# Batch normalisation at inference: stores on ScalarE's queue, one transfer at a time on each ring

## The chip, the cores and the metric

The kernel runs on one core of a Trainium2 chip. The metric is the device time of one execution in microseconds (us). A core has several engines that run side by side: ScalarE (ACT), VectorE (DVE), GpSimd (POOL), SyncE (SP) and TensorE, which has no work here. Sixteen DMA engines move data between the chip's main memory (HBM) and the core's on-chip memory of 128 partitions. An engine issues a transfer on a queue of its own; in the DMA engines that queue is a ring, and the profile numbers the rings q1 (SyncE), q10 (ScalarE) and q0 (GpSimd).

## The reference

```
x: float32 [32, 256, 128, 128]      gamma, beta, mean, var: float32 [256]
out = gamma * (x - mean) / sqrt(var + 1e-5) + beta        (per channel)
```

For each channel this is one multiplication and one addition: `scale = gamma / sqrt(var + eps)`, `shift = beta - mean * scale`, `out = x * scale + shift`. The input has 536.9 MB and the output as much.

## The kernel before

The 256 channels make two blocks of 128, one channel to a partition. An image and a block give a tile of 128 rows with 128 x 128 = 16384 numbers each, 64 KB a row and 8.4 MB a tile. There are 32 x 2 = 64 tiles (`NT`). Three buffers of that size (`bufs`, `NBUF = 3`) lie in on-chip memory; tile `i` uses buffer `i % 3`, and the result is written over the input in place.

At the start SyncE issues the first tile in two halves, with the four small parameter loads between them, and then tiles 1 and 2 (L89 to L98). VectorE and ScalarE work out `scale_t` and `shift_t` (L108 to L127). The main work is written out by hand, engine by engine:

- SyncE issues the loads of tiles 3 to 63 in order (L158 to L163). Load `i` waits on `stored[s]`, the semaphore that the store of tile `i - 3` raises when it has left the buffer.
- ScalarE applies scale and shift to the whole tile in one instruction (`scalar_part`, L142) when it has landed, for all tiles but the first and the last.
- GpSimd issues the stores of tiles 0 to 60 (L172), each when ScalarE has finished its tile (`adone`). The last three stores (`NTAIL`) are issued by ScalarE.
- VectorE (`vector_part`, L131) does the left half of tile 0 and the first 9216 columns of tile 63, and nothing in between.

Nothing else orders the transfers: a load may stand on its ring behind another load, a store behind another store. At the end GpSimd and SyncE wait for all stores.

Of the kernel before, what the change touches and what calls it, by code (L numbers as in the profile page):

```python
# [8 lines left out]
NBUF = 3  # L9
PAD = 936  # L10
NHEAD = 3
NTAIL = 3
VHEAD = 8192
VLAST = 9216


@with_exitstack
def kernel(
    ctx: ExitStack,
    tc: tile.TileContext,  # L20
    x: bass.AP,
    gamma: bass.AP,
    beta: bass.AP,
    running_mean: bass.AP,
    running_var: bass.AP,
    out: bass.AP,
):
    nc = tc.nc
    eps = 1e-5
    f32 = mybir.dt.float32  # L30

    N, C, H, W = x.shape
    P = nc.NUM_PARTITIONS
    assert C % P == 0
    NCB = C // P
    HW = H * W
    NT = N * NCB
    B = 32
    NQ = P // B
    NE = 16  # L40
    NPAR = 4

    xr = x.rearrange("n (cb p) h w -> (n cb) p (h w)", p=P)
    outr = out.rearrange("n (cb p) h w -> (n cb) p (h w)", p=P)

    params = ctx.enter_context(tc.tile_pool(name="params", bufs=1))
    data = ctx.enter_context(tc.tile_pool(name="data", bufs=1))
    params.tile([P, PAD], f32, name="pad", tag="pad")
    bufs = [data.tile([P, HW], f32, name=f"t{s}", tag=f"t{s}") for s in range(NBUF)]
    rows = params.tile([B, NPAR * C], f32, name="rows", tag="rows")  # L50
    turned = params.tile([B, NPAR * C], f32, name="turned", tag="turned")
    par = params.tile([P, NPAR, NCB], f32, name="par", tag="par")
    eps_t = params.tile([P, 1], f32, name="eps_t", tag="eps")
    std_t = params.tile([P, NCB], f32, name="std_t", tag="std")
    rstd_t = params.tile([P, NCB], f32, name="rstd_t", tag="rstd")
    scale_t = params.tile([P, NCB], f32, name="scale_t", tag="scale")
    ms_t = params.tile([P, NCB], f32, name="ms_t", tag="ms")
    shift_t = params.tile([P, NCB], f32, name="shift_t", tag="shift")

    loaded = [tc.alloc_semaphore(f"loaded{s}") for s in range(NBUF)]
    stored = [tc.alloc_semaphore(f"stored{s}") for s in range(NBUF)]
    closed = [tc.alloc_semaphore(f"closed{s}") for s in range(NBUF)]
    early = tc.alloc_semaphore("early")
    first = [tc.alloc_semaphore(f"first{s}") for s in range(NHEAD)]
    vdone = tc.alloc_semaphore("vdone")
    adone = tc.alloc_semaphore("adone")
    fetched = tc.alloc_semaphore("fetched")
    vec = tc.alloc_semaphore("vec")  # L70
    act = tc.alloc_semaphore("act")

    with tc.tile_critical():  # L73
        count = [0]

        def step(inst, sem=None, value=None):
            if sem is not None:
                inst._wait_ge(sem, value)
            elif count[0]:
                inst._wait_ge(vec, count[0])  # L80
            inst.then_inc(vec, 1)
            count[0] += 1
            return count[0]

        left, right = slice(0, HW // 2), slice(HW // 2, HW)
        last = NT - 1


        nc.sync.dma_start(out=bufs[0][:, left], in_=xr[0][:, left]).then_inc(early, 16)  # L89
        zeroed = step(nc.vector.memset(rows[:], 0.0))  # L90
        for r, ap in enumerate((running_var, gamma, beta, running_mean)):
            inst = nc.sync.dma_start(out=rows[0:NE, r * C : (r + 1) * C], in_=ap.partition_broadcast(NE))  # L92
            if r == 0:
                inst._wait_ge(vec, zeroed)
            inst.then_inc(fetched, 16)
        nc.sync.dma_start(out=bufs[0][:, right], in_=xr[0][:, right]).then_inc(first[0], 16)  # L96
        for i in range(1, NHEAD):
            nc.sync.dma_start(out=bufs[i][:], in_=xr[i]).then_inc(first[i], 16)  # L98

        def landed(i):  # L100
            if i < NHEAD:
                return first[i], 16
            s = i % NBUF
            before = 1 if s < NHEAD else 0
            return loaded[s], 16 * (i // NBUF + 1 - before)


        step(nc.vector.memset(eps_t[:], eps))  # L108
        step(nc.vector.transpose(out=turned[:], in_=rows[:]), fetched, 16 * NPAR)  # L109
        blocks = turned.rearrange("p (rc q b) -> p rc q b", q=NQ, b=B)  # L110
        flat = par.rearrange("p r cb -> p (r cb)")
        for q in range(NQ):
            placed = step(nc.vector.tensor_copy(out=flat[q * B : (q + 1) * B], in_=blocks[:, :, q, 0]))  # L113
        var_t, gamma_t, beta_t, mean_t = (par[:, r] for r in range(NPAR))
        nc.scalar.activation(  # L115
            out=std_t[:],
            in_=var_t,
            func=mybir.ActivationFunctionType.Sqrt,
            bias=eps_t[:],
            scale=1.0,  # L120
        )._wait_ge(vec, placed).then_inc(act, 1)
        step(nc.vector.reciprocal(out=rstd_t[:], in_=std_t[:]), act, 1)  # L122
        step(nc.vector.tensor_mul(out=scale_t[:], in0=gamma_t, in1=rstd_t[:]))  # L123
        step(nc.vector.tensor_mul(out=ms_t[:], in0=mean_t, in1=scale_t[:]))  # L124
        ready = step(nc.vector.tensor_sub(out=shift_t[:], in0=beta_t, in1=ms_t[:]))  # L125
        nc.vector.wait_ge(vec, ready)
        nc.scalar.wait_ge(vec, ready)  # L127

        def vector_part(i, first_col, end):
            t, cb = bufs[i % NBUF], i % NCB  # L130
            return nc.vector.tensor_scalar(  # L131
                out=t[:, first_col:end],
                in0=t[:, first_col:end],
                scalar1=scale_t[:, cb : cb + 1],
                scalar2=shift_t[:, cb : cb + 1],
                op0=mybir.AluOpType.mult,
                op1=mybir.AluOpType.add,
            ).then_inc(vdone, 1)

        def scalar_part(i, first_col):  # L140
            t, cb = bufs[i % NBUF], i % NCB
            return nc.scalar.activation(  # L142
                out=t[:, first_col:],
                in_=t[:, first_col:],
                func=mybir.ActivationFunctionType.Identity,
                bias=shift_t[:, cb : cb + 1],
                scale=scale_t[:, cb : cb + 1],
            ).then_inc(adone, 1)


        def share(i):
            return VHEAD if i == 0 else VLAST if i == last else 0

        vector_part(0, 0, HW // 2)._wait_ge(early, 16)
        vector_part(last, 0, VLAST)._wait_ge(*landed(last))


        for i in range(NHEAD, NT):  # L158
            s = i % NBUF
            inst = nc.sync.dma_start(out=bufs[s][:], in_=xr[i])  # L160
            if i >= NBUF:
                inst._wait_ge(stored[s], 16 * (i // NBUF))
            inst.then_inc(loaded[s], 16)  # L163

        for i in range(NT):
            eng = nc.gpsimd if i < NT - NTAIL else nc.scalar
            packet = {"single_packet": True} if i < NT - NTAIL else {}
            written = (stored if i < NT - NTAIL else closed)[i % NBUF]
            scalar_part(i, share(i))._wait_ge(*landed(i))
            if i in (0, last):  # L170
                eng.wait_ge(vdone, 1 if i == 0 else 2)
            eng.dma_start(out=outr[i], in_=bufs[i % NBUF][:], **packet)._wait_ge(adone, i + 1).then_inc(  # L172
                written, 16
            )


        for s in range(NBUF):
            nc.gpsimd.wait_ge(stored[s], 16 * ((NT - NTAIL - s + NBUF - 1) // NBUF))
        nc.gpsimd.drain()

        for s in range(NBUF):
            nc.sync.wait_ge(stored[s], 16 * ((NT - NTAIL - s + NBUF - 1) // NBUF))
            nc.sync.wait_ge(closed[s], 16)


# [28 lines left out]
```

## Time and profile before

| | |
|---|---|
| median of 3 runs | 2508.89 us (2481.34 to 2515.49) |
| span of the profiled execution | 2479.7 us |
| ScalarE busy | 885.6 us (36%), 66 instructions |
| VectorE busy | 13.1 us (1%), 13 instructions |
| GpSimd busy | 32.7 us (1%), 65 instructions |
| moved by DMA | 1073.84 MB, 433 GB/s on average |
| load, issue to landing | 55.3 us (median of 63) |
| store from GpSimd, issue to landing | 46.2 us (median of 61) |

The span runs from the first to the last instruction of the profiled execution. That execution has no other time on record; the lowest of the three runs is 1.6 us above its span. "Busy" counts instructions that compute; the issue of a transfer is not counted on SyncE and ScalarE. Issue to landing includes the time for which a transfer stands on its ring behind the one before it.

### The profile page before, as it was taken

How to read it: one execution, taken by the hardware profiler on the slowest of the kernel's cores; microseconds unless marked ns; L12 is line 12 of the kernel's file. 1: busy time of each engine (PE TensorE's matmuls, PEld its weight loads, DVE VectorE, ACT ScalarE, POOL GpSimd, SP SyncE). 2: the span in 40 equal slices, each digit the busy share in tenths (PEclk: the TensorE clock that was granted, in tenths of full speed). 3: DMA queues.
4: the chain of work that ended last, by engine and by line, in shares of the span. 5: the costliest groups of instructions: out<-in, count | busy, mean ns of one | idle time of the engine just before them, and what ended most of it. 6: DMA issues, size and time to landing. Idle time of an engine off the chain costs nothing.

```text
span 2479.7 us, 276 instructions
## 1 busy us (share of the span) xinstructions
DVE 13.1 (1%) x13; ACT 885.6 (36%) x66; POOL 32.7 (1%) x65
## 2 busy tenths in 40 slices
DVE  1000000000000000000000000000000000000000
ACT  2342432424424234242342433424334243342432
POOL 0000000000000000000000000000000000000000
DMA  9999999999999999999999999999999999999999
GB/s 410 437 440 426 437 440 428 434 440 432 430 440 432 430 440 433 429 440 436 427 440 436 427 440 437 426 440 437 426 440 437 426 440 438 425 440 438 425 440 406
DMA packets 18707, 1073.84 MB, mean 433 GB/s; under 512 B 2128, under 2 KB 2192, under 8 KB 2192
## 3 DMA queue, kind: packets, MB, share of 16 engines
q1 hardware_dynamic: 9488, 536.94, 50.0%
q0 software_dynamic: 8784, 511.71, 47.6%
q10 hardware_dynamic: 432, 25.17, 2.3%
q14 instruction: 3, 0.02, 0.0%
HBM read 536.94 MB, written 536.87 MB: 433 GB/s over the span
## 4 chain that ended last, share of the span: by engine, by line
another core or an unknown queue 61%; ACT 35%; DMA 2%; issue 0%; SPq 0%; DVE 0%; ACTq 0%; DVEq 0%
ACT t L142 35%; DMA t<-in_x_dram 2%; SPq L92 0%; DVE rows L90 0%; ACTq L172 0%; SPq L96 0%; DVE eps_t L108 0%; DVEq L209 0%; SPq L73 0%
## 5 line engine op out<-in xcount | busy, mean ns | idle before, releaser
L142 ACT ACTIVATE t<-t,shift_t,scale_t 128x16384 f32<-128x16384 f32 (+1 forms) x64 | 884.0, 13813 | 1554.8 <-DMA t<-in_x_dram 1554.8
L172 POOL DMA_DIRECT2D out_dram<-t x61 | 32.5, 534 | 2314.4 <-ACT t L142 2314.4
L131 DVE TENSOR_SCALAR t<-t,scale_t,shift_t 128x8192 f32<-128x8192 f32 (+1 forms) x2 | 9.6, 4812 | 2427.1 <-DMA t<-in_x_dram 2427.0
L115 ACT ACTIVATE std_t<-par,eps_t 128x2 f32<-128x2 f32 x1 | 0.3, 295 | 14.0 <-DVE par L113 14.0
L115 ACT ACT_TABLE_LOAD x1 | 1.3, 1283 | 0.9 <-SPq L73 0.9
L109 DVE STREAM_TRANSPOSE turned<-rows 32x1024 f32<-32x1024 f32 x1 | 1.2, 1233 | 11.9 <-DMA rows<-in_running_mean_dram 11.9
L90 DVE MEMSET rows<- 32x1024 f32 x1 | 0.9, 912 | 1.2 <-SPq L73 1.2
L113 DVE COPY par<-turned 32x8 f32<-32x8 f32 x4 | 0.6, 162 | 0.1
L122 DVE RECIPROCAL rstd_t<-std_t 128x2 f32<-128x2 f32 x1 | 0.2, 166 | 0.4 <-ACT std_t L115 0.4
L124 DVE TENSOR_TENSOR ms_t<-par,scale_t 128x2 f32<-128x2 f32 x1 | 0.2, 163 | 0.0
L125 DVE TENSOR_TENSOR shift_t<-par,ms_t 128x2 f32<-128x2 f32 x1 | 0.2, 161 | 0.0
L123 DVE TENSOR_TENSOR scale_t<-par,rstd_t 128x2 f32<-128x2 f32 x1 | 0.2, 160 | 0.0
L198 POOL MEMSET const-float32-0.0<- 128x1 f32 x1 | 0.1, 98 | 0.2 <-issue 0.2
L198 POOL MEMSET const-bfloat16-1.0<- 128x1 bf16 x1 | 0.1, 101 | 0.0
L198 POOL MEMSET const-float32-1.0<- 128x1 f32 x1 | 0.1, 98 | 0.0
L198 POOL MEMSET const-uint8-127<- 128x1 uint8 x1 | 0.1, 98 | 0.0
L108 DVE MEMSET eps_t<- 128x1 f32 x1 | 0.1, 59 | 0.1
## 6 DMA issues: line engine op xcount, KB each, us to landing
t<-in_x_dram SPq DMA_DIRECT2D x2, 4096.0 KB, 15.9
t<-in_x_dram SPq DMA_DIRECT2D x63, 55.3
out_dram<-t POOLq DMA_DIRECT2D x61, 46.2
out_dram<-t ACTq DMA_DIRECT2D x3, 32.2
rows<-in_running_var_dram SPq DMA_DIRECT2D x1, 16.0 KB, 11.3
rows<-in_gamma_dram SPq DMA_DIRECT2D x1, 16.0 KB, 11.1
rows<-in_beta_dram SPq DMA_DIRECT2D x1, 16.0 KB, 10.8
rows<-in_running_mean_dram SPq DMA_DIRECT2D x1, 16.0 KB, 10.7
```

What stands on the lines that cost most here:

```text
L90: zeroed = step(nc.vector.memset(rows[:], 0.0))
L109: step(nc.vector.transpose(out=turned[:], in_=rows[:]), fetched, 16 * NPAR)
L113: placed = step(nc.vector.tensor_copy(out=flat[q * B : (q + 1) * B], in_=blocks[:, :, q, 0]))
L115: nc.scalar.activation(out=std_t[:], in_=var_t, func=mybir.ActivationFunctionType.Sqrt, bias=eps_t[:], scale=1.0,)._wait_ge(vec, placed).t ...
L122: step(nc.vector.reciprocal(out=rstd_t[:], in_=std_t[:]), act, 1)
L123: step(nc.vector.tensor_mul(out=scale_t[:], in0=gamma_t, in1=rstd_t[:]))
L124: step(nc.vector.tensor_mul(out=ms_t[:], in0=mean_t, in1=scale_t[:]))
L125: ready = step(nc.vector.tensor_sub(out=shift_t[:], in0=beta_t, in1=ms_t[:]))
L131: return nc.vector.tensor_scalar(out=t[:, first_col:end], in0=t[:, first_col:end], scalar1=scale_t[:, cb : cb + 1], scalar2=shift_t[:, cb ...
L142: return nc.scalar.activation(out=t[:, first_col:], in_=t[:, first_col:], func=mybir.ActivationFunctionType.Identity, bias=shift_t[:, cb : ...
L172: eng.dma_start(out=outr[i], in_=bufs[i % NBUF][:], **packet)._wait_ge(adone, i + 1).then_inc(written, 16)
L198: nc = _bacc.Bacc("TRN2", target_bir_lowering=False, num_devices=1)
```

## The change

Three things change, and one follows from them.

1. All stores are issued by ScalarE, on its ring; GpSimd issues none, and the separate semaphores for the last three stores go. `gone(i)` names the semaphore and the value that say that tile `i` is stored.
2. VectorE takes part in each tile from tile 1 on: first columns 0 to 2559 (`VFIRST`), which raises `vfirst`, then columns 2560 to 14335 (`VMOST`; to 9215 for the last tile), which raises `vdone`. ScalarE does the rest, the last 2048 columns. A store waits for both engines.
3. From tile 3 on, SyncE issues load `i` when tile `i - 3` is stored and when VectorE has done the first part of tile `i - 1`, which means that load `i - 1` has landed. ScalarE starts its part of tile `i` only when tile `i - 1` is stored, for all tiles but the first and the last two. So in most of the run the load ring holds one load and the store ring one store.

```diff
-NTAIL = 3
+VFIRST = 2560
+VMOST = 14336
...
-        def share(i):
-            return VHEAD if i == 0 else VLAST if i == last else 0
-
-        vector_part(0, 0, HW // 2)._wait_ge(early, 16)
-        vector_part(last, 0, VLAST)._wait_ge(*landed(last))
+        def gone(i):
+            return stored[i % NBUF], 16 * (i // NBUF + 1)
+
+        vector_part(0, 0, VHEAD)._wait_ge(early, 16).then_inc(vdone, 1)
+        for i in range(1, NT):
+            vector_part(i, 0, VFIRST)._wait_ge(*landed(i)).then_inc(vfirst, 1)
+            vector_part(i, VFIRST, VLAST if i == last else VMOST).then_inc(vdone, 1)
 
         for i in range(NHEAD, NT):
             s = i % NBUF
-            inst = nc.sync.dma_start(out=bufs[s][:], in_=xr[i])
-            if i >= NBUF:
-                inst._wait_ge(stored[s], 16 * (i // NBUF))
-            inst.then_inc(loaded[s], 16)
+            nc.sync.wait_ge(*gone(i - NBUF))
+            nc.sync.dma_start(out=bufs[s][:], in_=xr[i])._wait_ge(vfirst, i - 1).then_inc(loaded[s], 16)
 
         for i in range(NT):
-            eng = nc.gpsimd if i < NT - NTAIL else nc.scalar
-            packet = {"single_packet": True} if i < NT - NTAIL else {}
-            written = (stored if i < NT - NTAIL else closed)[i % NBUF]
-            scalar_part(i, share(i))._wait_ge(*landed(i))
-            if i in (0, last):
-                eng.wait_ge(vdone, 1 if i == 0 else 2)
-            eng.dma_start(out=outr[i], in_=bufs[i % NBUF][:], **packet)._wait_ge(adone, i + 1).then_inc(
-                written, 16
+            if 0 < i < NT - 2:
+                nc.scalar.wait_ge(*gone(i - 1))
+            scalar_part(i, VHEAD if i == 0 else VLAST if i == last else VMOST)._wait_ge(*landed(i))
+            nc.scalar.wait_ge(vdone, i + 1)
+            nc.scalar.dma_start(out=outr[i], in_=bufs[i % NBUF][:])._wait_ge(adone, i + 1).then_inc(
+                stored[i % NBUF], 16
             )
```

More of the change, by code (lines that the diff above doesn't have):

```diff
@@ L137, in vector_part @@
                 op1=mybir.AluOpType.add,
-            ).then_inc(vdone, 1)
+            )
         def scalar_part(i, first_col):
```

10 lines of the change are left out of this document (3 added, 7 removed).

## The prediction

> **What bounds the kernel now.** I read the page's counts and queues first, then the instruction groups by shape, then the queue's own waits, then single windows.
>
> ```profile
> span 2479.7 us, 276 instructions
> DVE 13.1 (1%) x13; ACT 885.6 (36%) x66; POOL 32.7 (1%) x65
> DMA packets 18707, 1073.84 MB, mean 433 GB/s; under 512 B 2128, under 2 KB 2192, under 8 KB 2192
> q1 hardware_dynamic: 9488, 536.94, 50.0%
> q0 software_dynamic: 8784, 511.71, 47.6%
> q10 hardware_dynamic: 432, 25.17, 2.3%
> ```
>
> The last three lines give, for each ring, the share of the span of all 16 DMA engines that its packets took: loads on SyncE's ring q1 50.0%, GpSimd's stores on q0 47.6%, the last three stores on ScalarE's ring q10 2.3%. The sum is 99.9%. No compute engine is busy for over 36%. The DMA engines have 0.1% of 2479.7, some 2.5 us, left to win; more would need the same bytes to go faster than 433 GB/s.
>
> ```profile
> 100.00:2300.00 2200.00, 0.00 (x0) 797.95 (x58) 30.28 (x57) 1.00 1.00 434
> 4.00:31.00 27.00, 7.08 (x10) 7.51 (x2) 0.00 (x1) 1.00 1.03 438
> 0.00:1.00 1.00, 0.00 (x0) 0.09 (x1) 0.20 (x4) 1.00 0.00 0
> 1.00:2.00 1.00, 0.78 (x1) 1.00 (x1) 0.00 (x0) 1.00 0.49 131
> 2.00:3.00 1.00, 0.19 (x2) 0.19 (x1) 0.00 (x0) 1.00 1.26 393
> ```
>
> These are windows; the last two columns are DMA share and GB/s (a packet is counted where it starts, so short windows overshoot). Over 2200 us the share is 1.00 with both rings filled. From 4 to 31 us loads run alone, and one ring moves 438 GB/s: a lone ring gets the whole of the engines. The first three windows price a restart: the first load is issued at 0.96, no byte moves before 1.0 and the rate is there only within the third window, so issue to flow takes 1.0 to 1.8 us.
>
> ```profile
> SPq L160 <- DMA out_dram<-t: 2369.7, 61, 69.4
> ACT t L142 <- DMA t<-in_x_dram: 1554.8, 64, 27.2
> t<-in_x_dram SPq DMA_DIRECT2D x63, 55.3
> out_dram<-t POOLq DMA_DIRECT2D x61, 46.2
> ```
>
> SyncE's queue waits for stores to free a buffer, ScalarE for loads. A buffer's round is 55.3 (load) + 14.0 (compute) + 46.2 (store) = 115.5 us for three tiles, 38.5 a tile; successive computes in the trace stand 38.6 apart. So a load overlaps its successor on its ring by 55.3 - 38.6 = 16.7 us and a store by 7.6: neither ring ever runs dry, and that is why 99.9% is reached.
>
> **The change, part by part.** *Compute.*
>
> ```profile
> L142 ACT ACTIVATE t<-t,shift_t,scale_t 128x16384 f32<-128x16384 f32 x62 | 870.5, 14040 | 1525.3 <-DMA t<-in_x_dram 1525.3
> L142 ACT ACTIVATE t<-t,shift_t,scale_t 128x8192 f32<-128x8192 f32 x1 | 7.2, 7212 | 7.0 <-DMA t<-in_x_dram 7.0
> L142 ACT ACTIVATE t<-t,shift_t,scale_t 128x7168 f32<-128x7168 f32 x1 | 6.4, 6360 | 22.6 <-DMA t<-in_x_dram 22.6
> L131 DVE TENSOR_SCALAR t<-t,scale_t,shift_t 128x9216 f32<-128x9216 f32 x1 | 5.1, 5079 | 2427.0 <-DMA t<-in_x_dram 2427.0
> L131 DVE TENSOR_SCALAR t<-t,scale_t,shift_t 128x8192 f32<-128x8192 f32 x1 | 4.5, 4546 | 0.1
> ```
>
> ScalarE costs (7212-6360)/1024 = 0.832 ns a column and 0.40 us fixed, so 2048 columns take 2.10 us. VectorE costs 533/1024 = 0.52 ns a column and 0.28 us fixed, so 2560 columns take 1.61 us and the other 11776 take 6.41 us. ScalarE loses 62 x 11.9 = 740 us of work, VectorE gains 62 x 8.0 = 497. Neither is on the path: both lie under 38.6 us of transfers a tile. Without that cover a tile would cost 8.0 us on VectorE.
>
> *Stores from GpSimd to ScalarE.* Sixty-one issues of 0.53 us (GpSimd) become issues of 0.34 us on ScalarE: 21 us on an engine that has 23 us of idle time or more in each tile, so nothing. What is queued behind a store on ScalarE is only the next tile's ring wait, and it needs that store anyway. The store must also wait for VectorE's second part, 8.0 us after landing; the store ring is then still in the middle of the tile before, which hides it. GpSimd's closing waits and drain go, off the path. In the windows 31 to 41 us, where GpSimd's first store starts, the trace shows 419 GB/s against 434: 10 us x 15/434 = 0.35 us that a ScalarE start may save. I take -0.5, bounds -1 to 0.
>
> *The ring waits.* SyncE issues load i only when store i-3 is gone and VectorE has done the first 2560 columns of tile i-1, so behind that wait stand the next loads alone. ScalarE starts its last 2048 columns only when store i-1 is gone; behind it stand its store and the next tile. So each ring drains once a tile. The load ring's gap is 0.1 to 0.4 us for the semaphore (in the timeline GpSimd's issue follows ScalarE's end by 0.3), 1.61 of VectorE, and the restart of 1.0 to 1.8: 2.7 to 3.8 us. The store ring's is the same with 2.10 of ScalarE: 3.2 to 4.3 us. Work that hides it: the other ring's transfer, which takes all the engines while it is alone (438 GB/s above). What matters is that the two gaps do not fall together. At the point where the regime begins, store 0 is gone at 74.8 (the trace's first later load issue), so store 1 starts near 77 to 79; load 2 lands a little before 91.6, so load 3 starts near 90 to 94. The gaps are 12 to 16 us apart in a tile of 38.6, and each lies well inside the other's transfer. So the engines stay filled.
>
> Do they stay apart? If the engines shared time continuously, the ring with the shorter gap would gain twice the difference, 2 x (2.10 - 1.61) = 1.0 us a tile, and the gaps would meet after some 12 to 16 tiles. But the engines work by packets: 8 rows of 64 KB for each engine in a tile, each 65536 B / (433/16 GB/s) = 2.42 us. A gap costs whole turns. Both estimated gaps lie between one and two packets (2.42 and 4.84 us), so both rings give up the same number of turns and the offset holds. That is the choice on which the forecast rests. Price of all 61 gaps: 0 us; ends: 0 when they are hidden, and 61 x 4.3 = 262 us when each falls on idle engines.
>
> *The tail.* The last two stores have no ring wait. In the trace the last load lands at 2449.0, the last store is issued at 2455.4 and the store before it ends at about 2458.6, a margin of 3.2 us. With the rings interleaved otherwise, the last load can land one packet later or earlier (2.42 us), which uses up or leaves this margin. I take +1.5, bounds 0 to 4.
>
> Sum: 2479.7 - 0.5 + 1.5 + 0 = 2480.7 us of span. The runs before go from 2481.3, 1.6 above the profiled span, to 2515.5, with a median 29.2 above it; no row says where the 28 to 34 us come from, so no row says whether the change keeps them. If it keeps none the time is 2482, if it keeps all it is 2510; I take the middle, 2496.
>
> A rule of the Trainium skill bears on the ceiling: "DMA: Bandwidth & Descriptors", section "Where 436 GB/s comes from", puts the limit of the fabric at 435.2 GB/s; by it 1073.84 MB take an estimated 2467 us and no change of queues goes below that. The trace has 433.
>
> **The rivals.** *Drift and collision (slower).* If one gap takes two turns and the other three, which a restart some 0.6 us longer than the first load's would do for the store ring alone, loads gain on stores until load i waits for store i-3. Then one event, a store's end, releases both rings: the load after a restart, the store after 2.10 us more, and the engines idle meanwhile. From the rows the idle time is 1.1 to 2.2 us until the load flows, and up to 4.3 until both do; with 16 engines that don't finish together I take 4.2 a tile. All 61 tiles: 2479.7 + 256 = 2736. By the slow drift, colliding after 15 tiles: 46 x 4.2 = 193, 2673. It decides as soon as the mean idle time passes 50/61 = 0.8 us a tile (2%). For it: the gaps differ by 0.5 us, nothing pulls the offset back, and a restart on loaded engines isn't shown by any row. Against it: the whole turns, and the wide offset at the start.
>
> *Each restart is seen in part.* Rings never meet, but engines that finish early wait for the last one, and a lone ring does not fill every turn at its start: 61 x 1.0 to 1.8 = 61 to 110 us, 2541 to 2590, middle 2566. Against it: 438 GB/s with one ring. The Trainium skill, "DMA: Bandwidth & Descriptors", section "Anatomy of one DMA — SWDGE (gpsimd) path", gives each DMA a fixed cost of about 2.0 us, mostly completion; taken as uncovered once a tile it would make an estimated 2602. The trace before hides it, since both rings hold a next transfer there.
>
> *The rate rises (faster).* With fewer transfers open, engines could keep the rate of the page's best slices, 440 GB/s: 1073.84/440 = 2441 us. Against it: packets fill 99.9% already, and the slices swing only by where starts are counted.
>
> *The waits never bind.* Then nothing but the issuing queue changes, 2480. Against it: overlaps of 16.7 and 7.6 us on the rings, which the waits must cut. The time would be the forecast's.
>
> **How the numbers follow.** Forecast, with the waits that never bind: 0.55. Drift and collision: 0.32. Seen in part: 0.08. Rate: 0.05. A measurement of this kernel tells about 2% from no change, so faster is below 2459 and slower above 2559. The forecast's own range is 2478 to 2516. Faster 0.05; same 0.55 plus 0.02 of the partial case (its low end), 0.57; slower 0.38. The range must reach into the collision: 2478 to 2738.
>
> **What would show it.** Right: the queues' shares still add up to over 99%, each load's issue-to-landing falls from 55.3 to 35 to 37 us and each store's from 46.2 to 35 to 37, the starts of ScalarE's parts stay 38.6 to 38.7 apart, and SyncE waits for VectorE's first part (L131's helper), not for a store. Wrong: tiles 42 to 43 us apart, SyncE's queue released by stores and ScalarE's by the same event, slices of the GB/s row near 390 with an onset in time (drift) or throughout. A steady 39.5 to 40.5 a tile with loads released by VectorE would be the partial case. VectorE's 2560-column groups should show 1.6 us, ScalarE's 2048 2.1.

## The result, and the profile after

The changed kernel takes 2486.3 us (median of 22 runs, 2483.5 to 2487.2). The kernel before, run beside it, took 2504.0 (22 runs, 2481.3 to 2517.6). The ratio is 0.9947, with a 95% interval of 0.9923 to 0.9971: half a per cent faster in this set of runs. The two sets of runs differ in kind. Before, the runs lie in two groups, near 2481 to 2482 and from 2493 to 2518; after, all lie within 3.7 us. The shortest run before is 2.2 us shorter than the shortest after. The change does not make a good execution shorter; it takes the long ones away.

Span, queues and issues on the page of the changed kernel:

```profile
span 2485.4 us, 578 instructions
q1 hardware_dynamic: 9488, 536.94, 50.0%
q10 hardware_dynamic: 9216, 536.88, 49.9%
out_dram<-t ACTq DMA_DIRECT2D x64, 36.5
t<-in_x_dram SPq DMA_DIRECT2D x63, 37.0
```

The shares still add up to 99.9%. Both medians are now below the 38.6 us of a tile, so neither ring holds a second transfer any more. Groups by shape:

```profile
L132 DVE TENSOR_SCALAR t<-t,scale_t,shift_t 128x11776 f32<-128x11776 f32 x62 | 397.2, 6407 | 0.0
L143 ACT ACTIVATE t<-t,shift_t,scale_t 128x2048 f32<-128x2048 f32 x62 | 129.8, 2093 | 2250.8 <-DMA out_dram<-t 2243.3 <-DMA t<-in_x_dram 7.5
L132 DVE TENSOR_SCALAR t<-t,scale_t,shift_t 128x2560 f32<-128x2560 f32 x63 | 101.6, 1612 | 1938.7 <-DMA t<-in_x_dram 1938.7
```

The three durations are those that were worked out (6.41, 2.10, 1.61 us). SyncE's queue, by what it waited for:

```profile
SPq L163 <- DMA out_dram<-t: 1693.3, 61, 69.3
SPq L164 <- DVE t L132: 689.5, 61, 11.4
```

Line 163 is the wait for the buffer, line 164 the load with its wait for VectorE. Each of the 61 loads waits first for a store and then, 11 us more, for VectorE: it is VectorE that releases them. The timeline, cut to one store issue and the next load issue at the start, in the middle and near the end:

```profile
76.89 0.34 ACTq L171 DMA_DIRECT2D out_dram<-t  x1
...
86.00 39.09 SPq L164 DMA_DIRECT2D t<-in_x_dram  x2
...
1200.99 0.34 ACTq L171 DMA_DIRECT2D out_dram<-t  x1
...
1210.11 77.61 SPq L164 DMA_DIRECT2D t<-in_x_dram  x3
...
2362.71 0.34 ACTq L171 DMA_DIRECT2D out_dram<-t  x1
...
2371.84 39.27 SPq L164 DMA_DIRECT2D t<-in_x_dram  x2
```

A load is issued 9.11 us after a store at the start, 9.12 in the middle and 9.13 near the end; over all 61 loads it is 9.1 to 9.2. The rings do not drift.

### The profile page after: what moved, and what is told of

It is laid out like the page before. It is cut to its first block, busy times and chain, and to the rows that moved or that the text cites. A ratio compares the mean times of both kernels' runs of the same rounds, so it can differ in the third digit from the quotient of the medians.

```text
span 2485.4 us, 578 instructions
## 1 busy us (share of the span) xinstructions
DVE 505.3 (20%) x138; ACT 144.9 (6%) x66; POOL 0.2 (0%) x4
## 4 chain that ended last, share of the span: by engine, by line
DMA 93%; DVE 4%; another core or an unknown queue 1%; ACT 0%; issue 0%; SPq 0%; DVEq 0%
DMA t<-in_x_dram 93%; DVE t L132 4%; ACT t L143 0%; SPq L93 0%; DVE rows L91 0%; SPq L97 0%; DVE eps_t L109 0%; DVEq L203 0%; SPq L74 0%
## 5 line engine op out<-in xcount | busy, mean ns | idle before, releaser
L132 DVE TENSOR_SCALAR t<-t,scale_t,shift_t 128x11776 f32<-128x11776 f32 (+2 forms) x127 | 501.8, 3993 | 1938.8 <-DMA t<-in_x_dram 1938.7
L143 ACT ACTIVATE t<-t,shift_t,scale_t 128x2048 f32<-128x2048 f32 (+1 forms) x64 | 143.3, 2239 | 2299.2 <-DMA out_dram<-t 2243.3
```

Source lines behind the costliest of these rows:

```text
L132: return nc.vector.tensor_scalar(out=t[:, first_col:end], in0=t[:, first_col:end], scalar1=scale_t[:, cb : cb + 1], scalar2=shift_t[:, cb ...
L143: return nc.scalar.activation(out=t[:, first_col:], in_=t[:, first_col:], func=mybir.ActivationFunctionType.Identity, bias=shift_t[:, cb : ...
```

## The experiments

Two questions were asked. What removes the long executions: the queue, the ring waits or the new shares of the engines? And is it a count of packet turns that holds the rings apart?

**The queue alone** (the kernel before):

```diff
-            eng = nc.gpsimd if i < NT - NTAIL else nc.scalar
-            packet = {"single_packet": True} if i < NT - NTAIL else {}
+            eng = nc.scalar
+            packet = {}
...
-
-        for s in range(NBUF):
-            nc.gpsimd.wait_ge(stored[s], 16 * ((NT - NTAIL - s + NBUF - 1) // NBUF))
-        nc.gpsimd.drain()
```

With the stores, GpSimd's waits at the end go too.

> The kernel before, with all 64 stores on ScalarE's queue and nothing else changed: no ring waits, ScalarE still computes whole tiles. Theory Q (the runs of before are 12 to 36 us above its shortest because of GpSimd's queue): 2481 to 2487 us in every run, as steady as the change. Theory R (they are long because a ring holds two transfers at times): 2481 to 2517 with a median near 2504, as before. The profile should show loads at about 55 us and stores at about 46 us from issue to landing under both.

Twelve runs: seven from 2482.2 to 2483.3, one at 2489.2 and four from 2493.9 to 2504.6; the ratio to before is 0.9996 (0.9971 to 1.0022). The two groups remain, so theory Q falls. The Trainium skill, "DMA: Bandwidth & Descriptors", section "Rules for kernel authors", says that spreading transfers over issuing engines brings no bandwidth, since all run on the same DMA engines. Here the stores only change the engine that issues them, and the ratio shows no difference.

**No ring waits** (the changed kernel):

```diff
-            nc.sync.wait_ge(*gone(i - NBUF))
-            nc.sync.dma_start(out=bufs[s][:], in_=xr[i])._wait_ge(vfirst, i - 1).then_inc(loaded[s], 16)
+            nc.sync.dma_start(out=bufs[s][:], in_=xr[i])._wait_ge(*gone(i - NBUF)).then_inc(loaded[s], 16)
...
-            if 0 < i < NT - 2:
-                nc.scalar.wait_ge(*gone(i - 1))
```

> The changed kernel without both ring waits: a load waits only for its buffer, ScalarE's part only for its tile; queues and shares of the engines as in the change. Theory Q: 2481 to 2487 in every run. Theory R: spread from 2481 to 2517, median near 2504. A third theory S (what helps is the shorter time from landing to store, 8 us in place of 14) expects about 2486 here and about 2504 in the kernel that only moves the queue.

Median 2500.9, ratio 1.0021 (0.9990 to 1.0053), three runs from 2482.8 to 2483.6 and nine from 2495.2 to 2505.8. This is what theory R expected, and S falls: with queue and shares as in the change, the long executions come back when the waits go. The profiled execution was a long one (span 2500.0). Windows of it:

```profile
100.00:2300.00 2200.00, 444.37 (x112) 117.30 (x56) 0.00 (x0) 1.00 1.00 433
2462.00:2476.00 14.00, 5.27 (x2) 6.36 (x1) 0.00 (x0) 1.00 0.12 51
```

The long middle runs at full rate, and near the end the DMA engines are used for 12% during 14 us. The packet records say why. They name a packet's ring and not its engine, but on an engine one packet starts where another ends, so they can be put into sixteen chains; sums by engine are good to some 2 us. A packet of 64 KB takes 2.418 us, and some take longer, by 0.2 to 1.7 us; this is called excess below. In this execution two of the sixteen DMA engines collected 16 to 21 us of it, most others 4 to 6. The sixteen shares of a load, which complete within 3 us of each other in the first ten tiles, are 27 us apart from tile 36 on. At the end the last store waits for the last share of the last load, and the other engines stand idle. The kernel with the queue alone was profiled in a long execution too (span 2501.9): shares 22 us apart, excess of 10 to 24 us.

**Ring waits, stores on GpSimd's queue** (the changed kernel, stores 0 to 60):

```diff
-            nc.scalar.wait_ge(vdone, i + 1)
-            nc.scalar.dma_start(out=outr[i], in_=bufs[i % NBUF][:])._wait_ge(adone, i + 1).then_inc(
-                stored[i % NBUF], 16
+            eng = nc.gpsimd if i < NT - NBUF else nc.scalar
+            packet = {"single_packet": True} if i < NT - NBUF else {}
+            written = (stored if i < NT - NBUF else closed)[i % NBUF]
+            eng.wait_ge(vdone, i + 1)
+            eng.dma_start(out=outr[i], in_=bufs[i % NBUF][:], **packet)._wait_ge(adone, i + 1).then_inc(
...
```

The last three stores have semaphores of their own again (`closed`), and GpSimd's waits at the end are back.

> The changed kernel with both ring waits, but stores 0 to 60 on GpSimd's queue as before. Theory Q: long and scattered, median near 2504. Theory R: steady near 2486. Apart from both, GpSimd's start of a store is longer by 0.3 us or more, which could cost the store ring one packet turn more than the load ring; then the gaps meet and it is over 2600.

Seven runs, all from 2503.3 to 2510.3, ratio 1.0071 (1.0041 to 1.0101). Neither theory said this: steady, as with R, and long, as with Q. The shares stay within 5 us of each other; instead the store ring's packets carry 16.2 us of excess on an engine, on average, most of it 2 to 3 us after a store's issue. In the change ScalarE's ring has 2.4 us. So the queue matters once the ring drains every tile: on GpSimd's queue the store packets lose about 14 us more over 61 tiles, 0.23 us a store. The Trainium skill, "DMA: Bandwidth & Descriptors", section "Latency and other measured facts", puts the first byte at about 1 us for GpSimd's way of making descriptors and 0.6 for ScalarE's and SyncE's. The direction agrees; the excess here is nearer half of that difference. The first byte itself is not seen to come later: in both kernels a store's first packet follows its issue by 2.9 us (median).

**Longer and shorter gaps.** All are the changed kernel, whose `VFIRST` is 2560 and `VMOST` 14336, with other constants: late store, both late, both short and equal gaps, in this order below.

```diff
+VMOST = 11776     # late store

+VFIRST = 6912     # both late
+VMOST = 11776

+VFIRST = 1024     # both short
+VMOST = 15360

+VFIRST = 3456     # equal gaps
```

> The changed kernel with VectorE's second part ending at column 11776, so ScalarE does 4608 columns in 4.23 us in place of 2.10: the store ring's gap grows by 2.1 us, nearly one packet (2.42 us), the load ring's does not. Theory of whole turns: the store ring gives up one turn more per tile than the load ring, the gaps meet within some ten tiles, loads are then released by stores and not by VectorE, and the time is 2650 to 2800. If the rings simply fill in for each other whatever the gaps, it stays at 2486 to 2495.

2682.1 (2680.7 to 2683.6), ratio 1.0776 (1.0717 to 1.0835). As expected in time; but loads were still released by VectorE. The timeline around one tile, then the stage in a window and SyncE's wait for VectorE:

```profile
1210.65 0.34 ACTq L171 DMA_DIRECT2D out_dram<-t  x1
...
1212.76 84.22 SPq L164 DMA_DIRECT2D t<-in_x_dram  x3
```

```profile
100.00:2300.00 2200.00, 343.29 (x104) 221.84 (x53) 0.00 (x0) 1.00 0.97 400
SPq L164 <- DVE t L132: 402.2, 61, 13.7
```

The issues are 2.1 us apart in place of 9.1, so both rings are empty together. They start at 9.4 us, are 4.6 apart one tile later and 2.2 after one more, and stay there: the offset between the rings moved by two packets and then by one. Tiles are 42.0 us apart, and 400 GB/s are left of 433.

> The changed kernel with both gaps longer by about one packet: VectorE's first part has 6912 columns (3.9 us in place of 1.6), ScalarE's part 4608 (4.23 us in place of 2.10). Theory of whole turns: each ring gives up one turn more, the offset between the rings holds, and the time stays at 2484 to 2495, although the kernel with ScalarE's half of this alone took 2682. If instead a late store is bad in itself: 2680 or more.

Four runs: one at 2485.3, three from 2601.0 to 2605.3. The one run shows that late starts are not bad in themselves; the three, that this offset does not hold as the theory expected. In the profiled one (span 2602.5) tiles are in turn 39.4 and 42.0 us long and the issues 6.8 and 4.4 us apart, which is one packet of difference.

> The changed kernel with both gaps shorter by 0.8 us: VectorE's first part has 1024 columns (0.8 us), ScalarE's part 1024 (1.25 us). Whole turns: if both rings still give up the same number of turns, 2483 to 2487 and steady, with no drift between the starts of loads and stores; if one of them saves a turn, the gaps meet and it is over 2580.

2569.4 (2566.3 to 2572.7), ratio 1.0330 (1.0273 to 1.0386). The less favourable of the two cases, though under the 2580 that it named: tiles in turn of 38.8 and 41.4 us, 418 GB/s in the stage, and the issues 1.9 and 4.3 us apart. They start at 9.2 us and are 4.3 apart one tile later: again two packets at once.

> The changed kernel with VectorE's first part at 3456 columns (2.08 us in place of 1.61), so that the load ring's gap carries the same compute as the store ring's (2.10 us). If only the number of whole turns counts and both stay inside the same count: 2483 to 2488, steady, starts of loads and stores at a fixed distance. If the window is so narrow that 0.5 us on one side leaves it: 2540 or more, with loads released by stores or stores by landings.

2483.6, ten runs from 2482.3 to 2484.4. A load is issued 9.6 to 9.9 us after a store in all tiles but two; those two have 10.3, and the next tile has 9.6 again. It is the steadiest of all. In its set of runs before took 2481.7 (11 of 13 runs below 2483), ratio 0.9998 (0.9981 to 1.0015), so it is not shown to beat before; that it is 2.7 us below the change compares two sets of runs.

**One wait alone** (the changed kernel, the other wait taken out as in the kernel without ring waits).

> The changed kernel with the load ring's wait alone; a store waits only for its tile. Theory of whole turns: the load ring gives up three turns a tile and the store ring one or none, so stores gain on loads until a store waits for its own tile; then both rings are empty after a landing: above 2510, up to 2600. If either wait alone keeps the engines in step at no cost: 2484 to 2490.

2601.8 (2600.5 to 2603.1), ratio 1.0455 (1.0378 to 1.0532): the first theory, 2 us above its range. As it said, stores come to wait for their own tiles:

```profile
ACT t L143 <- DMA t<-in_x_dram: 2416.7, 64, 42.8
```

All of ScalarE's parts wait for a landing, and a landing also releases the next load. The stage moves 414 GB/s.

> The changed kernel with the store ring's wait alone; a load waits only for its buffer. Theory of whole turns: the store ring gives up turns and the load ring none, loads gain until every load waits for a store, and the end of a store releases both rings: 2680 to 2770, some 4 us a tile, as with the late store. If either wait alone keeps the engines in step at no cost: 2484 to 2490.

2712.6, one run. What SyncE and ScalarE waited for:

```profile
SPq L163 <- DMA out_dram<-t: 2601.8, 61, 69.7
ACT t L143 <- DMA out_dram<-t: 2471.7, 61, 44.5
```

This is the rival of collision in full. By its code a load here waits for a store alone; the trace adds that ScalarE's parts wait for a store too. One event, the end of a store, releases both rings: at one tile the load is issued at 1223.16 us, ScalarE's part starts at 1223.23 and its store is issued at 1225.35. The stage moves 395 GB/s. Each wait alone is about 100 us or more above the kernel with none (2500.9, in another set of runs). The waits work only as a pair.

**Both waits at every eighth tile:**

```diff
-            nc.sync.wait_ge(*gone(i - NBUF))
-            nc.sync.dma_start(out=bufs[s][:], in_=xr[i])._wait_ge(vfirst, i - 1).then_inc(loaded[s], 16)
+            if i % 8 == 7:
+                nc.sync.wait_ge(vfirst, i - 1)
+            nc.sync.dma_start(out=bufs[s][:], in_=xr[i])._wait_ge(*gone(i - NBUF)).then_inc(loaded[s], 16)
...
-            if 0 < i < NT - 2:
+            if i % 8 == 7:
```

> The changed kernel with both ring waits only at every eighth tile (i % 8 == 7), otherwise as without ring waits. Theory E (the sixteen DMA engines drift apart where nothing holds them together, and a wait for a whole transfer brings them back in step): one wait in eight is enough, 2482 to 2490 in all runs, and the completions of a load's sixteen shares stay within some 8 us of each other. Theory P (packets are slower while a ring holds two transfers): seven tiles in eight are as without waits, so 2483 to 2506 with a median near 2500.

2537.4 (2528.2 to 2542.0), ratio 1.0191 (1.0143 to 1.0238), worse than either theory. From tile 17 on the shares of a load are 15 to 19 us apart; at the waiting tiles it is 9.4 to 9.8, and 15 again at the next. Against the kernel without ring waits (2500.9, in another set of runs) it is 36 us more, some 4.6 for each of the eight waiting tiles. A single wait does not bring the engines back into step. Whether what it costs is the wait for the late engines or gaps that meet was not separated.

**The kernel before, profiled again:**

> The kernel before, unchanged, profiled once more to catch an execution of 2490 or more. Theory D (in its long executions a few DMA engines fall behind the others, one slow packet at a time): its last slices of the GB/s row drop well below the 406 of the short execution, near 350, the stage from 100 to 2300 us still moves 432 to 434 GB/s, and ScalarE's last wait for a load is longer by 10 to 20 us. If the rate were lower throughout, the stage would show 429 or less and the end nothing. A profile near 2480 tells neither.

> The same kernel once more, with the same expectations, in case the other profile is of a short execution.

Both caught long executions. The first (span 2496.7):

```profile
100.00:2300.00 2200.00, 0.00 (x0) 791.93 (x57) 30.28 (x57) 1.00 1.00 432
2480.00:2500.00 20.00, 0.00 (x0) 0.00 (x0) 0.00 (x0) 1.00 0.62 269
```

The second (span 2513.0):

```profile
100.00:2300.00 2200.00, 0.00 (x0) 792.49 (x57) 29.75 (x56) 1.00 1.00 430
2480.00:2500.00 20.00, 5.08 (x1) 6.36 (x1) 0.00 (x0) 1.00 0.70 301
```

Theory D is half right. The second has it: four engines collect some 30 us of excess and twelve 20 to 24, the shares of a load are 21 to 24 us apart from tile 30 on, and the end runs at 301 GB/s. ScalarE's last wait for a load, which should have grown by 10 to 20 us, is 22.3 us against 22.6 in the short execution. But the middle is slower as well, 430 against the 434 of the short execution, which makes 2200 x 4/434 = 20 us. In the first the shares of a load stay within 5 us up to tile 61 (6.5 and 9.0 for the last two) and those of a store within 8 (11.4 for tile 60), and every engine collects 13 to 18 us; its last window holds the program's end, so its 269 alone says little. Common to both are slow packets: 1247 and 826 over 2.43 us, against 28 in the short execution and 366 in the change. The count alone does not make an execution long: the long one without ring waits has 393, with a mean excess of 6.7 us on an engine, and the change 6.1. There two engines stand out (16 to 21 us against 4 to 6), in the change none does (5 to 7 us each).

## Why the prediction was right

The forecast was no gain at the DMA engines, rings that stay apart, and a time between 2482 and 2510 by how much of the runs' scatter the change keeps. It is 2486.3: it keeps none of the long executions. The 2496 that was named as the time is ten above it, as the middle of a term that no row decided.

*The floor* held. No kernel here had a run below 2481.1, and the shares stayed at 99.9%. The rival of a higher rate did not happen.

*Compute and issues at nothing* held. In the change ScalarE's part begins when a store ends (2243.3 us of its waiting), and no store waits for VectorE's second part but that of tile 62, which has no ring wait. The -0.5 for a quicker start on ScalarE does not show: from 31 to 41 us the change moves 419 GB/s, as before.

*The gap's size* was wrong, in two terms. The restart of 1.0 to 1.8 us came from the first load, on idle engines. With the other ring in flight, the first packet of a load follows its issue by 3.3 to 3.8 us in nearly all tiles (4.2 to 4.7 in the first few) and the sixteenth by about 6 (packet records). And the 0.1 to 0.4 us "for the semaphore" was read from one engine's wait for another, not for a transfer. A landing is a packet too, of 4 bytes, that takes its turn: it comes 2.75 us after the last packet of data beside a busy ring, and 0.3 us after it where the other ring is empty (the loads of the late store). So the load ring's gap is some 2.8 + 1.6 + 3.4 = 7.8 us, and the packets show it: a ring's last packet and its next first packet are 7.9 us apart on the load ring and 7.8 on the store ring in the middle of the run, not 2.7 to 4.3. So the gaps are longer than "between one and two packets (2.42 and 4.84 us)". That both rings give up the same number of turns came true, and it can be counted: on a single engine a ring's pause is mostly 9.66 us, four packets of the other ring, or 12.07, five, and its mean is 10.1 us on both rings. But it was not the number that the bounds gave; that two gaps, both sized at about half, came out equal is luck. The kernels with both gaps longer or both shorter, for which the same theory expected or allowed no loss, took about 116 us more (three of four runs) and 83.

*"The gaps are 12 to 16 us apart"* was too wide: the issues are 9.1 us apart. Load 2 landed at 84.3 us, not a little before the 91.6 of the trace before. As the gaps are near 8 us long, one begins 1.8 us after the other ends: in the tile at 1235 us the store ring is empty from 1234.65 to 1242.47 and the load ring from 1244.31 to 1252.20. That is a thin margin: 2.1 us more on one side cost 196 us. That 0.8 us less on both cost 83 does not follow from the margin; there the offset moved by two packets at the first tile.

*Drift and collision* was the right rival. Its place is as described: 42 us a tile, 395 to 400 GB/s. Its price of 2673 to 2736 holds the 2682 of the late store and the 2713 of the store wait alone. Its weaker form, every other tile longer by 2.6 us, was not foreseen, and where the gaps meet they do so within two or three tiles, by steps of whole packets, not by a slow drift over 12 to 16. "Nothing pulls the offset back" is too strong: with equal gaps a deviation of 0.7 us is gone one tile later. The continuous drift of 1.0 us a tile did not occur: the issues stay 9.1 to 9.2 us apart over 59 tiles.

*The tail* of +1.5 and the sum of 2480.7 missed 4.7 us: the profiled span is 2485.4. The packets of one engine add up to 2484.5 us on average, against 2479.1 before. So the 5.7 us by which the span grew are nearly all packets that take longer, 2.4 us of them on the store ring and 3.0 on the load ring, mostly 2 to 3 us after a store's issue and 4 to 15 us after a load's. The prediction had the gaps at 0; 5.4 us over 61 tiles is their price, far below the 61 to 110 us of the rival that sees each restart in part. The fixed cost of about 2.0 us for each DMA that the Trainium skill gives ("DMA: Bandwidth & Descriptors", section "Anatomy of one DMA — SWDGE (gpsimd) path", a fit for GpSimd's path) does not show in the time: once a tile it would have been an estimated 122 us.

*The scatter* was left undecided, and the middle was taken. The runs decide: without both waits executions are short or long, with both they are neither. Shown is that with the waits the excess is 5 to 7 us on every engine and the shares of a transfer stay within 5 us in the profiled execution, where without them an engine can collect from 10 to over 30 us. Not settled is why a packet takes longer, and why one execution of before has 28 of them and another 1247. The share of long executions also differs between the sets of runs: before had 16 of 22 runs at 2490 or more beside the change, 2 of 13 in the last set and 36 of 77 in all. The half per cent depends on that share.

## What to carry to other kernels

Where packets fill the DMA engines, a change of queues and waits can only win what the scatter between executions costs, so look at all runs before you look at the one that was profiled. Letting each ring hold one transfer keeps the engines in step, at about 5 us here, but only if both rings are held and their empty times do not meet: here one wait alone cost over 110 us against both, and 2 us of compute on one side almost 200. A restart or a landing measured on idle engines is no measure of one beside a busy ring.

## What the runs showed of the hardware

- A 64 KB packet on one DMA engine takes 2.418 us whether one ring has work or two; of 16256 such packets 28 took over 2.43 us in the short execution of before and 1247 in a long one.
- Two rings with work alternate packet by packet on an engine: in the short execution of before, from 100 to 2300 us, all 16384 neighbours are of different rings, with the 4-byte packet that ends a transfer counted as a turn. A landing came 2.75 us after the last packet of data beside a busy ring and 0.3 us after it beside an empty one.
- A ring that comes back beside a busy one got its first packet 3.3 to 3.8 us after the issue (SyncE) in most tiles; in the kernel with short gaps every other store, issued as a load ended, had its first packet on all sixteen engines 0.84 to 1.0 us after the issue.
- The sixteen DMA engines need not stay in step: shares of one load completed up to 27 us apart, and the last store then left most engines idle near the end (51 GB/s for 14 us).
- With one transfer at a time, a store on GpSimd's queue cost about 0.23 us more than on ScalarE's.
